# Output projection by Strassen's seven products from the third block on, prompt gates folded into w_out, and v weights streamed

## The chip, the core and the metric

The kernel runs on one core of one Trainium2 chip. The metric is the device time of one execution in microseconds (us), as the median of three runs. The engines are named as in the profile: PE is the matrix engine, PEld its loading of the stationary operand, DVE the vector engine, ACT the scalar engine, POOL the third elementwise engine, and SP the engine whose queue issues most of the DMAs.

## What is computed

One layer over 4096 prompt rows of 1024 channels (x_prompt) and over 8 x 16 sample rows (x_sample). What matters here is the frame around the mixers:

```python
mod = jax.nn.silu(c) @ w_ada + b_ada
shift, scale, gate = jnp.split(mod, 3, axis=-1)
h = rmsnorm(x, norm_g) * (1 + scale[:, None]) + shift[:, None]
z = h @ w_in                                   # 3200 columns: pool, conv, spatial-gating groups
...
vn = layernorm(v, v_norm_g, v_norm_b)          # v is one of the column groups, 384 wide
y_gmlp = gmlp_mix(u, vn, w_s, b_s)
y = jnp.concatenate([y_pool * jax.nn.silu(z_pool),
                     gb * y_conv * jax.nn.silu(z_conv),
                     y_gmlp * jax.nn.silu(z_gmlp)], axis=-1) @ w_out
return x + gate[:, None] * y, new_pool, new_conv, vn
...
y_prompt = rmsnorm(xp, final_norm_g)
```

All prompt rows share one conditioning vector, so the prompt's gate is one row of 1024 numbers; the sample rows have eight.

## The kernel before

The prompt is worked off in eight blocks of 512 rows (blocks 0 to 7), then the 128 sample rows follow as a ninth block ("dec"). Every float32 product is made of three float16 products: an operand is split into a high and a low part (`split`, L150: ACT writes the high part, DVE the low part), and `PARTS` lists the three pairs that are multiplied.

The order of the program is: input half of block i (`in_block`, or `in_dec`), preparation of the input of block i+1 (`h_plain`, `h_sums`), then the output half of block i-1 (`out_block`, L1101), and last the split of block i's result `ya` for its own output half one block later (`split_y`, L1145). So the output half of block 3 runs behind the input half of block 4, and the v product of block 5 follows it.

An input half multiplies first the v columns (`v_product`, L751: for each of four row tiles 24 matmuls of 384 columns, weights `vw` resident in SBUF), then the other columns in pairs of tiles. From block 1 (conv pairs: block 2) on these pairs use Strassen's seven products of half-sized operands (`quads`, L631): B11, T1, T2, B22, T3, B21, T4, 12 matmuls of 256 columns each, accumulated in three PSUM tiles x, y and z per pair. `gmlp_v` (L763) takes the four PSUM tiles `z_v`, normalises them on DVE and ACT and leaves `vh`, which the matmuls of `gmlp_mix` (`ps_mix`) read behind the first group of pairs.

The output half (`out_block`) computes 512 rows x 1024 columns in two column halves. For each half it opens four PSUM tiles `ps_o`, and for each of eight k tiles takes a weight tile from the stream and does 4 row tiles x 3 parts matmuls of 512 columns (L1173). DVE then does two operations per PSUM tile: times the scales and the gate (L1179), plus the residual `xr` (L1180). Row sums, a reciprocal root and the final scaling (L1189) follow, and ACT's queue stores the rows (L1190). `mid`, called between the halves, derives the scale of the next block's result. Block 7's output half (L1151) holds all 16 weight tiles and goes row tile by row tile.

Weights come through `Stream` (L196): a list of wanted tiles, loaded by SP in order into a ring of 18 slots of 256 KB, at most 16 tiles ahead of their use. A tile of w_out serves 12 matmuls before, a tile of a pair 12 matmuls too. SP issues in program order, and a load waits there for its buffer: `xt`, `xr` and the raw weights share the four tiles of the pool `xp`, which come free when the stores of `out_y` have landed.

In block 0 and block 1 the weights are split and stored to DRAM (`w_in_parts`, `w_out_parts`) for the later blocks; in block 1 also the gates are made (`ada_chunk`, `gates`: 16 tiles of w_ada through the stream). The order of instructions on each engine is made by a scheduler from the program's order; in parts of block 0 it is fixed by hand (`manual_schedule`, for SP in all of block 0).

## Time and profile before

| what | value |
|---|---|
| median of 3 runs | 1470.69 us (1470.62 to 1472.21) |
| the profiled execution's own time | 1467.08 us |
| its span, first to last instruction | 1465.3 us |
| mean granted clock of PE | 0.985 |
| PE busy | 1404.3 us (96%), 10370 matmuls |
| PEld busy | 975.9 us (67%) |
| DVE busy | 936.6 us (64%) |
| ACT busy | 585.0 us (40%) |
| HBM traffic | 214 GB/s over the span |

The span is one profiled execution; what lies around it (1.8 us) is part of the execution's time. A view by stretches gives each engine's busy time between two moments; a timeline gives groups of like instructions in order, with the idle time of the engine before them and what ended it in brackets.

### The profile page before, as it was taken

To read this page: it belongs to the slowest core of one execution; us is meant where nothing else is said; L and a number is where in the kernel's file an instruction comes from. 1 tells how busy PE (TensorE), PEld (TensorE's weight loads), DVE (VectorE), ACT (ScalarE), POOL (GpSimd) and SP (SyncE) were. 2 spreads that over 40 slices of the span, in tenths; PEclk is the share of its full clock that TensorE was granted. 3 is DMA by queue.
4 is the path that set the end of the run, shared out by engine and by line. 5 is a ranking of instruction groups with operands and counts; after the bars stand their busy time and mean duration, and the time that the engine had idled before them with its cause. 6 is when DMAs were issued, how large, how long until landed. Compare 5 with 4: busy or idle time off the path is not lost.

```text
span 1465.3 us, 26791 instructions
## 1 busy us (share of the span) xinstructions
PE 1404.3 (96%) x10370; PEld 975.9 (67%) x10370; DVE 936.6 (64%) x2073; ACT 585.0 (40%) x1166; POOL 119.6 (8%) x166
## 2 busy tenths in 40 slices
PE   5799999999999999999999999999999999999697
PEld 2454454584788658884788658874888568865663
DVE  3874696878887668465865657455845667354445
ACT  3676653553446434342533324342533234222121
POOL 0000202220020102000010002000200002000000
PEclk8999999999999999999999999999999999999999
DMA  9556737995559639685577639764776547774961
GB/s 352 207 222 230 280 110 258 343 361 163 209 182 356 219 129 330 174 279 159 213 242 200 187 116 321 194 184 158 263 214 200 155 139 243 204 214 125 230 179 58
DMA packets 155009, 315.08 MB, mean 215 GB/s; under 512 B 25217, under 2 KB 27009, under 8 KB 154881
## 3 DMA queue, kind: packets, MB, share of 16 engines
q1 hardware_dynamic: 143632, 295.28, 62.2%
q10 hardware_dynamic: 11248, 18.08, 3.6%
q8 instruction: 81, 1.33, 0.4%
q14 instruction: 48, 0.39, 0.1%
HBM read 267.06 MB, written 46.24 MB: 214 GB/s over the span
## 4 chain that ended last, share of the span: by engine, by line
PE 76%; DVE 10%; DMA 9%; ACT 2%; issue 1%; POOL 1%; SPq 0%; ACTq 0%; DVEq 0%; POOLq 0%
PE ps_o L1173 20%; PE zx L627 17%; PE zq L627 11%; PE zy L627 8%; PE z_v L757 7%; PE zz L627 5%; PE ps_o L1151 3%; DMA xt<-in_x 3%; PE z L627 2%; DVE mix L823 2%; DVE d L728 2%; DVE xr L1189 2%; DMA ws<-in_wada 1%; DMA raw<-in_win 1%; DMA ws<-w_in_parts 1%
## 5 line engine op out<-in xcount | busy, mean ns | idle before, releaser
L627 PEld LDWEIGHTS <-ws 128*128 128x128 f16 x6360 | 598.8, 98 | 114.6 <-issue 18.9
L1173 PE MATMUL ps_o<-ws,yh 128*128 128x512 f16 x1344 | 291.9, 379 | 0.0
L1173 PEld LDWEIGHTS <-yh 128*128 128x128 f16 x1344 | 131.0, 98 | 155.8
L627 PE MATMUL zy<-S,ws 128*128 128x256 f16 x1572 | 184.2, 273 | 0.0
L627 PE MATMUL zx<-A,ws 128*128 128x256 f16 x1572 | 183.4, 273 | 0.2 <-DVE np L659 0.2
L627 PE MATMUL zx<-S,ws 128*128 128x256 f16 x1440 | 168.8, 273 | 9.6 <-ACT nzg L655 6.7
L627 PEld LDWEIGHTS <-wp 128*128 128x128 f16 x1056 | 103.1, 98 | 74.8 <-issue 7.6
L757 PE MATMUL z_v<-vw,A 128*128 128x384 f16 x792 | 132.7, 330 | 1.9 <-ACT A L310 1.7
L627 PE MATMUL zq<-A,wp 128*128 128x512 f16 x528 | 117.3, 383 | 0.0
L757 PEld LDWEIGHTS <-A 128*128 128x128 f16 x792 | 77.8, 99 | 55.7 <-ACT A L310 2.5
L153 ACT ACTIVATE yh<-ya,sy 128x512 f16<-128x512 f32 x64 | 40.7, 708 | 166.2 <-PE ps_o L1173 162.5
L1179 DVE SCALAR_TENSOR_TENSOR ps_o<-ps_o,io,gate_p 128x512 f32<-128x512 f32 x56 | 40.9, 751 | 102.9 <-PE ps_o L1173 102.9
L627 PE MATMUL zz<-A,ws 128*128 128x256 f16 x852 | 101.5, 273 | 0.0
L627 PE MATMUL zq<-A,ws 128*128 128x512 f16 x288 | 62.6, 379 | 0.0
L711 POOL COPY qh<-q 128x2 f32<-128x2 f32 x24 | 6.6, 273 | 559.1 <-DVE q L710 559.1
L701 DVE SCALAR_TENSOR_TENSOR c<-q,wconv_sb,c 128x512 f32<-128x512 f32 (+1 forms) x54 | 38.0, 704 | 21.7 <-ACT c L699 21.1
L714 ACT ACTIVATE nzc<-nzc 128x512 f32<-128x512 f32 x24 | 15.1, 628 | 80.9 <-DVE nzc L659 80.8
L823 DVE SCALAR_TENSOR_TENSOR mix<-ps_mix,wsg,wsb 64x256 f32<-64x256 f32 x96 | 46.3, 482 | 1.4
L154 DVE SCALAR_TENSOR_TENSOR yh<-ya,sy,yh 128x512 f16<-128x512 f32 x64 | 44.9, 740 | 0.0
L627 PE MATMUL z<-A,ws 128*128 128x128 f16 x588 | 37.7, 228 | 5.9 <-ACT sz L1034 5.4
L725 POOL TENSOR_TENSOR pw<-pw 128x524 f32<-128x524 f32 (+5 forms) x36 | 42.6, 1183 | 8.1 <-DVE d L728 5.8
L741 POOL COPY ph<-pe 128x15 f32<-128x15 f32 x16 | 3.7, 232 | 476.6 <-ACT pe L740 476.3
(277 smaller groups left out, 1739.0 us busy)
## 6 DMA issues: line engine op xcount, KB each, us to landing
ws<-w_in_parts SPq DMA_DIRECT2D x517, 256.0 KB, 3.1
ws<-w_out_parts SPq DMA_DIRECT2D x128, 256.0 KB, 3.5
w_in_parts<-wp SPq DMA_DIRECT2D x83, 256.0 KB, 4.3
t<-in_xT SPq DMA_DIRECT2D x32, 512.0 KB, 6.0
xr<-in_x SPq DMA_DIRECT2D x32, 512.0 KB, 7.2
out_y<-xr ACTq DMA_DIRECT2D x32, 512.0 KB, 3.9
xt<-in_x SPq DMA_DIRECT2D x28, 512.0 KB, 6.1
ws<-in_wada SPq DMA_DIRECT2D x48, 256.0 KB, 5.4
```

Source lines behind the costliest of these rows:

```text
L153: nc.scalar.activation(dst_hi, src, AF.Identity, scale=s)
L154: nc.vector.scalar_tensor_tensor(dst_lo, src, s, dst_hi, ALU.mult, ALU.subtract)
L627: nc.tensor.matmul(ps, w[:, a, k, :], h[:, c, k, :], start=first and i == 0, stop=last and i == 3 * KH - 1, skip_group_check=True)
L701: nc.vector.scalar_tensor_tensor(c, at(i), wc[:, j, i:i + 1], c, ALU.mult, ALU.add)
L725: nc.gpsimd.tensor_tensor(cut(s, lo), cut(sums[-1], lo), cut(sums[-1], lo - w, -w), ALU.add)
L728: nc.vector.scalar_tensor_tensor(dv[rows], cut(sums[e], 16)[rows], state["G"]["cinv"][rows, i:i + 1], cut(pe, 16)[rows], ALU.mult, ALU.sub ...
L757: nc.tensor.matmul(ps, H[1 + k // KH][:, a, k % KH, t * P:(t + 1) * P], vw[:, e, k, :], start=i == 0, stop=i == 3 * KT - 1)
L823: nc.vector.scalar_tensor_tensor(mo[to, :, t, :], po[of, :, e, :], gc[of, hd:hd + 1], bias[of, hd, :].unsqueeze(1).broadcast_to([64, 2, P] ...
L1151: nc.tensor.matmul(ps, yh[:, a, k, t * P:(t + 1) * P], state["w"][hf][k][:, c, 0, :], start=k == 0 and i == 0, stop=k == KT - 1 and i == 2)
L1173: nc.tensor.matmul(pss[t], yh[:, a, k, t * P:(t + 1) * P], w[:, c, 0, :], start=k == 0 and i == 0, stop=k == KT - 1 and i == 2)
L1179: nc.vector.scalar_tensor_tensor(pss[t], pss[t], io[:, hf:hf + 1], gate[:, hs], ALU.mult, ALU.mult)
L1189: nc.vector.scalar_tensor_tensor(xts[t], xts[t], r[:, t:t + 1], O["fg"], ALU.mult, ALU.mult)
```

## The change

1. From block 2 on (`OUT_FAST`) the output half of a prompt block uses Strassen's seven products too (`out_fast`): operands of the result's split are seven sums of its quarters (`split_y_fast`), and weights are plain tiles or the four sums of w_out's quarters, which block 3 makes once and stores (`out_sums`). Each product has 4 k tiles x 2 row tiles x 3 parts matmuls of 512 columns. Three PSUM pairs x, y, z are accumulated across products, and DVE adds what stands in them to the residual after each product. The final row work (`out_rows`) stands behind the seventh product; in block 7 half of it stands behind the sixth.
2. The prompt's gate is multiplied into w_out in block 1 (`out_bounds`), so DVE does one operation per PSUM read where it did two. The sample rows need w_out without gates, which block 5 makes (`later`). The gates themselves are made in block 0 now. The high part of w_out's split is written by ACT, not POOL.
3. The split v weights are stored to DRAM in the first 40 us and come through the stream, eight tiles of 192 KB for each block; `v_products` goes k tile by k tile over four PSUM tiles that end together.
4. Weight jobs move: `unfold` from block 3 to block 4, `out_sums` into block 3, the plain w_out into block 5.

```diff
+    def v_products(b, H):
+
+        pss = [psum("z_v")[:, :384] for _ in range(b.tt)]
+        for k in range(KT):
+            w = stream.get()[:, :768].rearrange("p (a c) -> p a c", a=2)
+            for t in range(b.tt):
+                for i, (a, e) in enumerate(PARTS):
+                    nc.tensor.matmul(pss[t], H[1 + k // KH][:, a, k % KH, t * P:(t + 1) * P], w[:, e, :],
+                                     start=k == 0 and i == 0, stop=k == KT - 1 and i == 2)
+            stream.ahead(1)
+        return pss
...
         for i in range(3):
             cols = slice(i * P, (i + 1) * P)
             split(vw[:, 0, :, cols], vw[:, 1, :, cols], t[:, i, :].rearrange("p (k c) -> p k c", k=KT), s)
+        for k in range(KT):
+            nc.sync.dma_start(wvd[k].rearrange("p (a c) -> p a c", a=2), vw[:, :, k, :])
...
+    def out_bounds(hf, sts, gate=None):
+
+        m = sm.tile([P, 4], F32, tag="wom", name="wom", bufs=1)
+        for q, st in enumerate(sts):
+            if gate is not None:
+                nc.vector.tensor_tensor(st, st, gate.unsqueeze(1).broadcast_to([P, 2, 512]), ALU.mult)
+                nc.sync.dma_start(wofd[hf][:, 2 * q:2 * q + 2, :], st)
+            bound(m[:, q:q + 1], st, 4.0)
+        return m
...
+    def out_sums(k, a, c):
+
+        (_, s1), (_, s2) = state["O"]["inv"]
+        r11, r12, r21, r22 = a[:, 0], a[:, 1], c[:, 0], c[:, 1]
+        stt = nc.vector.scalar_tensor_tensor
...
+        nc.scalar.activation(r11, r11, AF.Identity, scale=s1)
+        nc.vector.tensor_tensor(r22, r22, r12, ALU.subtract)
+        stt(r12, r12, s2, r11, ALU.mult, ALU.subtract)
+        out(0, r12)
+        stt(r11, r22, s2, r11, ALU.mult, ALU.add)
+        out(1, r11)
+        out(2, r22, s2)
+        stt(r21, r21, s1, r11, ALU.mult, ALU.subtract)
+        out(3, r21)
...
+                if b.i == 0 and j > 0:
+                    gates(j - 1, ada_chunk(stream.get), state["O"])
...
-                if b.i == 1 and j < 2:
-                    t = ada_chunk(stream.get)
-                    out_weights(j, state["O"], *wo)
-                    if j == 0:
-                        wo = out_load(1)
-                    gates(j, t, state["O"])
...
+    def split_y_fast(ya, sy):
+
+        y11, y21, y12, y22 = ya[:, :KH, :HT], ya[:, :KH, HT:], ya[:, KH:, :HT], ya[:, KH:, HT:]
+        Ya = hop.tile([P, 4, 2, KH, HT], F16, tag="yh", name="yh")
+        Yb = hop.tile([P, 3, 2, KH, HT], F16, tag="yh2", name="yh2")
+        op = {B11: Ya[:, 0], T1: Ya[:, 1], T2: Ya[:, 2], B22: Ya[:, 3], T3: Yb[:, 0], B21: Yb[:, 1], T4: Yb[:, 2]}
+        split(op[B11][:, 0], op[B11][:, 1], y11, sy)
+        split(op[T4][:, 0], op[T4][:, 1], y22, sy)
+        nc.vector.tensor_tensor(y22, y21, y22, ALU.add)
+        split(op[T1][:, 0], op[T1][:, 1], y22, sy)
+        nc.vector.tensor_tensor(y21, y11, y21, ALU.subtract)
+        split(op[T3][:, 0], op[T3][:, 1], y21, sy)
+        nc.vector.tensor_tensor(y11, y22, y11, ALU.subtract)
+        split(op[T2][:, 0], op[T2][:, 1], y11, sy)
+        split(op[B21][:, 0], op[B21][:, 1], y12, sy)
+        nc.vector.tensor_tensor(y12, y12, y11, ALU.subtract)
+        split(op[B22][:, 0], op[B22][:, 1], y12, sy)
+        return op
...
+    def out_fast(b, op, io, xts, mid):
+
+        pss = {}
+        reads = {B11: (0, 0), T1: (1, 1), T2: (0, 1), B22: (0, 1), T3: (1, 1), B21: (0, 0), T4: (1, 0)}
+        for p in (B11, T1, T2, B22, T3, B21, T4):
+            bank = "y" if p in (T1, B22) else "z" if p == B21 else "x"
...
+            for k in range(KH):
+                w = as_parts(stream.get(), 512)
+                for t in range(2):
+                    for i, (a, c) in enumerate(PARTS):
+                        nc.tensor.matmul(pss[bank][t], op[p][:, a, k, t * P:(t + 1) * P], w[:, c, 0, :],
...
+                stream.ahead(1)
+            half, hf = reads[p]
+            hs = slice(hf * 512, hf * 512 + 512)
+            for t in range(2):
+                xt = xts[2 * half + t][:, hs]
+                nc.vector.scalar_tensor_tensor(xt, pss[bank][t], io[:, hf:hf + 1], xt, ALU.mult, ALU.add)
+            if p == T2:
+                mid()
+            if b.last and p in (B21, T4):
+                out_rows(b, xts, (2 * half, 2 * half + 1))
+        if not b.last:
+            out_rows(b, xts, range(TB))
...
     for i in range(1, NPB):
-        stream.want += in_items(i) + wod
-    stream.want += dec_items() + wod
+        stream.want += in_items(i) + out_items(i - 1)
+    stream.want += dec_items() + out_items(NPB - 1) + wosd
```

Three places show how instructions stand now. The first is DVE behind the output half of block 3, up to the first reading of the next v product. Before, from the last matmuls of `ps_o`'s second half on (`yh` is the split result of block 4, `z_v` the v product of block 5):

```order
L1179 SCALAR_TENSOR_TENSOR ps_o<-ps_o,io,gate_p 128x512
L154 SCALAR_TENSOR_TENSOR yh<-ya,sy,yh 128x512
L1180 TENSOR_TENSOR xr<-ps_o,xr 128x512
L154 SCALAR_TENSOR_TENSOR yh<-ya,sy,yh 128x512 x2
L1180 TENSOR_TENSOR xr<-ps_o,xr 128x512
L154 SCALAR_TENSOR_TENSOR yh<-ya,sy,yh 128x512
L774 BN_STATS bst<-z_v 128x6
L154 SCALAR_TENSOR_TENSOR yh<-ya,sy,yh 128x512 x4
```

The same place now, from the reading of the seventh product (`ox`) on:

```order
L1246 SCALAR_TENSOR_TENSOR xr<-ox,io,xr 128x512 x2
L161 SCALAR_TENSOR_TENSOR yh_10049<-ya,sy,yh_10049 128x1024 x2
L1200 TENSOR_TENSOR ya<-ya 128x4x256
L1219 TENSOR_SCALAR omsq_10017<-oss 128x4
L1202 TENSOR_TENSOR ya<-ya 128x4x256
L129 TENSOR_SCALAR rs_t<-omsq_10017 128x4
L133 TENSOR_SCALAR rs_y<-omsq_10017 128x4
L161 SCALAR_TENSOR_TENSOR yh<-ya,sy,yh 128x1024
L1204 TENSOR_TENSOR ya<-ya 128x4x256
L131 TENSOR_SCALAR rs_r<-rs_t 128x4
L161 SCALAR_TENSOR_TENSOR yh_10049<-ya,sy,yh_10049 128x1024
L1207 TENSOR_TENSOR ya<-ya 128x4x256
```

Two more splits of 128x1024 follow before the four `BN_STATS` of `z_v`, which stood amid the splits before and stand behind all of them now; the four scalings of `xr` (L1222) stand between them and the reading of `z_v` that frees its PSUM tiles, as L1189 did.

The second place is SP's queue around the same v product, where `xt` waits for the stores of the block before. Before:

```order
L217 DMA ws<-w_out_parts 128x1024 x16
L217 DMA ws<-w_in_parts 128x1024 x8
L295 DMA t<-in_xT 128x1024 x4
L217 DMA ws<-w_in_parts 128x1024 x10
L238 DMA xt<-in_x 128x1024
```

Now (behind the 28 weight tiles of the output half):

```order
L302 DMA t<-in_xT 128x1024
L224 DMA ws<-w_v_parts 128x768
L224 DMA ws<-w_in_parts 128x1024 x22
L245 DMA xt<-in_x 128x1024
L224 DMA ws<-w_in_parts 128x1024 x2
```

Eight loads of v weights came in, and the first `xt` stands behind 22 tiles of the next pairs where it stood behind 18.

The third place is SP's queue in the first 45 us, whose order is fixed by hand. Before (`t` is the input of block 0, the first `raw` are the v weights, the second the weights of the first conv pairs):

```order
L295 DMA t<-in_xT 128x1024 x4
L491 DMA raw_148<-in_win 128x1024 x3
L217 DMA ws<-in_wada 128x512 x16
L399 DMA raw<-in_win 128x1024 x4
L592 DMA gate_p<-in_badag 128x512 x2
```

Now:

```order
L302 DMA t<-in_xT 128x1024 x4
L497 DMA raw_147<-in_win 128x1024 x3
L224 DMA ws<-in_wada 128x512 x16
L513 DMA w_v_parts<-vw 256x1x384 x8
L405 DMA raw<-in_win 128x1024 x4
```

The eight stores of the split v weights stand ahead of the raw weights of the first conv pairs.

## Rows read from the trace of the kernel before

**Rows 1.** The page: busy time (share) and instructions of engines; chain by engine.
```profile
PE 1404.3 (96%) x10370; PEld 975.9 (67%) x10370; DVE 936.6 (64%) x2073; ACT 585.0 (40%) x1166; POOL 119.6 (8%) x166
...
PE 76%; DVE 10%; DMA 9%; ACT 2%; issue 1%; POOL 1%; SPq 0%; ACTq 0%; DVEq 0%; POOLq 0%
```

**Rows 2.** Timeline of PE behind block 4's input half: start, us, group [idle before].
```profile
839.41 20.88 PE L1173 MATMUL ps_o<-ws,yh 128*128 128x512 f16 x96
860.12 15.76 PE L757 MATMUL z_v<-vw,A 128*128 128x384 f16 x96
875.73 2.78 PE L627 MATMUL zx<-A,ws 128*128 128x256 f16 x24
...
888.83 2.78 PE L627 MATMUL zz<-A,ws 128*128 128x256 f16 x24
...
894.07 1.50 PE L816 MATMUL ps_mix<-wmix,vh 128*128 128x128 f16 x24
```

**Rows 3.** Stretches: us, PE, PEld, DVE, ACT, POOL busy, PEclk, DMA share, GB/s.
```profile
698.41:860.10 161.69, 160.51 (x1254) 121.07 (x1253) 99.72 (x209) 58.26 (x119) 10.57 (x16) 1.00 0.65 204
...
875.90:894.20 18.30, 18.30 (x171) 16.40 (x170) 14.31 (x46) 10.85 (x22) 3.29 (x6) 1.00 1.02 379
```

**Rows 4.** Timelines of PE and DVE in blocks 0 and 1, around the gates.
```profile
114.69 0.16 PE L145 MATMUL ps_sum<-asum,ones 128*128 128x1 bf16 x1 [3.11 <-DVE asum L143]
228.58 1.92 PE L273 MATMUL ps_ada<-ws,c_sb 128*32 128x512 f32 x16
231.29 1.98 PE L594 MATMUL ps_gate<-t_ada,ex 128*128 128x512 f32 x4 [0.67 <-ACT t_ada L276]
...
113.10 0.38 DVE L556 MEMSET st_ws<- 64x384 f32 x1 [7.03 <-DMA st_ws<-in_wsT]
```

**Rows 5.** Groups by line, DVE: forms, count, busy us, mean ns, idle before.
```profile
L1179 DVE SCALAR_TENSOR_TENSOR ps_o<-ps_o,io,gate_p 128x512 f32<-128x512 f32 x56 | 40.9, 751 | 102.9 <-PE ps_o L1173 102.9
L347 DVE TENSOR_TENSOR t<-t 128x1024 f32<-128x1024 f32 x7 | 8.5, 1217 | 0.0
L154 DVE SCALAR_TENSOR_TENSOR vw<-raw,w_s,vw 128x1024 f16<-128x1024 f32 x3 | 3.7, 1282 | 1.2 <-ACT vw L153 1.2
L774 DVE BATCH_NORM_STATS2 bst<-z_v 128x6 f32<-128x384 f32 x33 | 18.2, 551 | 1.4 <-PE z_v L757 1.4
...
L133 DVE TENSOR_TENSOR rs_q<-rs_q,rs_y 128x4 f32<-128x4 f32 x45 | 8.9, 197 | 1.2
...
L133 DVE TENSOR_TENSOR rs_q<-rs_q,rs_y 128x2 f32<-128x2 f32 x48 | 7.4, 154 | 0.6
```

**Rows 6.** Timeline of DVE behind the same output half.
```profile
872.89 4.87 DVE L1189 SCALAR_TENSOR_TENSOR xr<-xr,rs_r,fgain 128x1024 f32<-128x1024 f32 x4
...
880.40 1.26 DVE L786 TENSOR_SCALAR v<-z_v,va,vb 128x384 f32<-128x384 f32 x2
...
885.86 1.26 DVE L786 TENSOR_SCALAR v<-z_v,va,vb 128x384 f32<-128x384 f32 x2
```

**Rows 7.** Timeline of SP's queue, the first xt of block 5.
```profile
877.28 0.33 SPq L238 DMA_DIRECT2D xt<-in_x  x1
```

**Rows 8.** Timelines of SP's queue, DVE and ACT in the first 53 us.
```profile
31.34 2.36 SPq L399 DMA_DIRECT2D raw<-in_win  x4
...
34.59 3.68 DVE L154 SCALAR_TENSOR_TENSOR vw<-raw,w_s,vw 128x1024 f16<-128x1024 f32 x3 [1.16 <-ACT vw L153]
...
52.83 1.04 ACT L162 ACTIVATE junk<-raw 128x1024 bf16<-128x1024 f32 x1
```

**Rows 9.** Input half of the sample rows: PE, SP's queue, and its stretch (columns of Rows 3).
```profile
1384.76 0.62 PE L807 MATMUL ps_mix<-wmix_s,vh 128*128 128x128 f16 x3 [4.34 <-ACT gc L1022]
...
1392.70 1.97 PE L627 MATMUL z<-A,ws 128*128 128x128 f16 x17 [5.45 <-ACT sz L1034]
...
1374.48 0.33 SPq L1109 DMA_DIRECT2D xr<-in_x  x1
...
1348.07:1405.63 57.56, 45.57 (x684) 43.14 (x683) 30.24 (x80) 17.71 (x49) 3.46 (x7) 0.88 0.96 236
```

202 lines of the change are left out of this document (123 added, 79 removed).

## The prediction

> **What bounds the kernel now.** I read the page first: PE is busy for 96% of the span, every other engine for less than two thirds, and the chain that ended last runs through PE for 76% [rows 1]. A busy PE need not be a PE without slack, so the second view is PE's timeline where the change sits, behind the input half of block 4 [rows 2]: an output half is two groups of 96 matmuls, the v product follows without a gap, and the first pairs of block 5 follow that. No group there has an idle time in brackets. From the start of the second half (839.41) to the start of the v product (860.12) 20.71 us pass, so one matmul of 512 columns costs 20.71/96 = 0.216 us from start to start; the 20.88 of the row holds the modelled end of the last one as well. The third view is the stretch of a whole block: 161.69 us with PE busy for 160.51, at a granted clock of 1.00, the 2.4 GHz level [rows 3]. The middle blocks are therefore PE's issue rate and little else; a matmul that goes away there shortens the run by its spacing, unless something new is late. Only at the start [rows 4, 8] and in the input half of the sample rows [rows 9] does PE wait for others.
>
> **What is removed from PE.** Before, an output half is 2 x 8 x 4 x 3 = 192 matmuls; seven products are 7 x 4 x 2 x 3 = 168. Six blocks (2 to 7) lose 24 each: 144 x 0.216 = **31.1 us**. Size and stationary operand of a matmul stay, the clock is at its upper level there, so I take the spacing as it is.
>
> The Trainium skill, TensorE: Matmul & The Clock Gate, section Back-to-back issue gap, gives two figures for the spacing of matmuls of 512 columns: about 216 ns by its formula for the bare gap, and about 131 ns as measured in a stream with weight loads between. By the second the saving would be 144 x 0.131 = 18.9 us, an estimate; the trace has 0.216 in just such a stream, so it bears out the first.
>
> **Gates, from block 1 to block 0.** In block 1 two chunks cost 1.92 + 1.98 us each on PE plus a wait of 0.67 [rows 4], together 9.1 us. They cost the same in block 0, but the first one now stands where PE waited 3.11 us for a chain that began with a late DMA of `st_ws` (DVE idle 7.03 us) [rows 4]. The PE work of 3.9 us covers most of that wait, and the DMA moves back by two issues only. I take **-2.4 us**, from -3.1 (all covered) to +1 (the two loads ahead of `st_ws` push the chain by as much as they fill).
>
> **DVE and ACT at the seam between two blocks.** This is where new waits can come. Per read of PSUM DVE has one operation of 0.75 us [rows 5] where it had two, and 14 reads where it had 8; that is even. But the split of `ya` grows: seven splits of 128x1024, nearest row 1.28 us on DVE, and four additions, nearest row 1.22 us [rows 5]. The order shows what of it cannot begin early: T4's operand overwrites a tile that the seventh product still reads, and T1, T3, T2 and B22 depend on `ya` as changed after it. So behind the seventh product stand two reads (1.5 us), six splits (7.7), four additions (4.9) and some eight small operations (about 1.3): 15.4 us on DVE. PE meanwhile does the rest of the v product, 15.6 us in all. DVE reaches `BN_STATS` when PE ends v, not before.
>
> From there the same chain as now runs: statistics, small operations, four scalings of `xr` (4.87 us [rows 6]), then the reads that free `z_v`. Before they began at 880.40 and 885.86 [rows 6], 4.7 and 10.1 us behind the end of v (875.73 [rows 2]), because half the statistics were done during v. Now I get 4 x 0.55 for the statistics, some 35 small ones at 0.15 to 0.2 [rows 5] and 4.87: 13 us for the first pair, about 21 for the second. PE wants PSUM again at the pair's `zz`, 13.1 us behind v's end (888.83 against 875.73), and `vh` at `ps_mix`, 18.3 us behind it (894.07) [rows 2]. PSUM holds eight tiles; x, y and `z_v` fill it, so `zz` waits for the first pair of reads: 0 to 2 us. The order puts half of `ps_mix` behind the next group of matmuls, which covers 2.6 us of the second delay; 1 to 2 us remain. Against it stands about 1.2 us of idle PE per block now (161.69 less 160.51 [rows 3]), part of which a wait upstream absorbs. I take 1.5 us at each of four seams (before blocks 4 to 7) and 1 us for blocks 1 to 3, where only v's order changes: **+7 us**, from 0 to +20 (5 us a seam, if ACT and DVE hand each split over without overlap: the `vw` row shows 1.2 us idle before the first of three [rows 5]).
>
> **Inside the output half** nothing should wait. Product T2 accumulates on what DVE must have read after B11, with T1 (5.2 us) between; likewise the others. Two reads of 0.75 us fit, and the order puts them in time.
>
> **Streams.** A block loads 12 more tiles of w_out and eight of v, 4.7 MB on 204 GB/s x 161.69 us = 33 MB [rows 3]; in 156 us that makes about 242 GB/s, below the 379 that the first pairs of a block reach [rows 3]. A w_out tile is used up in 1.3 us instead of 2.6, which is what pairs do now. The critical place is `xt`, which stops SP until `out_y` has landed, at 877.28 [rows 7], 1.5 us after v's end, with 18 tiles in the ring. Now v has used its tiles, and the stores start some 9 us later against v's end; 22 tiles are issued ahead of `xt`, about 8 used, so 14 remain, 18 us of work at 1.3. I cost it at nothing; if the cover goes, each missing tile costs its transfer, 256 KB at 379 GB/s, 0.7 us.
>
> **The rest.** *Start:* the v stores wait for the split, which ends at 38.3 [rows 8], and the raw weights behind them are issued near 43 (eight issues at some 0.6) instead of 31.34. They are first needed at 52.83 [rows 8]; 1.6 + 2.1 MB from 38.3 at 379 GB/s land by 49. +0.5 us, 0 to 4. *Weight jobs:* `out_sums` adds 4 x 8 operations of 0.75 = 24 us to DVE in block 3, plain w_out some 12 us in block 5; DVE has 62 us free in a block [rows 3]. PE may meet them at a few PSUM reads: +2 us, 0 to 8. *Sample rows:* here DMA is the limit, share 0.96 at 236 GB/s over 57.56 us while PE works 45.57, with waits of up to 4.34 and 5.45 us [rows 9]. Eight v tiles are 1.57 MB, 6.7 us at that rate. But SP's stop at `xr` (issued at 1374.48 [rows 9]) now has two tiles of the pairs behind it instead of ten, and the wait of 5.45 that followed it should go for the most part: +2 us, from -3 to +8. *End:* the row work of block 7 is hidden behind the sample rows' projection, as before: 0.
>
> **Sum.** -31.1 - 2.4 + 7 + 0.5 + 2 + 2 = -22.0 us. The profiled execution took 1467.08 (span 1465.3 and 1.8 around it), so 1445.1; the median of the runs shown is 3.6 above it, which makes **1449 us**.
>
> **Rivals.**
> 1. *The gain comes whole.* No new wait at the seams or in the sample rows, only the matmuls and the gates count: 1470.7 - 33.5 = 1437, to 1441 with small ones. For it: PE has no gap in the rows of the seam and its queue can pass other work; against it: the count of 15.4 us against 15.6. Chance 0.22.
> 2. *The forecast*, some waits, 1441 to 1456. Chance 0.58.
> 3. *DMA or DVE eats half.* Block 3 or 5 or the ring starves, 10 to 25 us in sum: 1456 to 1467.8. For it: a DMA share of 1.02 at the seam already [rows 3]; against it: 14 tiles in hand. Chance 0.12.
> 4. *A removed matmul is worth less than its row.* If the 24 that go from a block had been closer together than the others, their spacing might be that of the v product, 15.61/96 = 0.163 us [rows 2]: 144 x 0.163 = 23.4, 7.7 us less than I take, so 1457. Against it: 96 of one kind without a gap. Chance 0.02. The Trainium skill's 131 ns (TensorE: Matmul & The Clock Gate, Back-to-back issue gap) would put it later still, at 1461, an estimate.
> 5. *Slower.* The reads that free `z_v` come so late that `zz` waits about 9 us at each of four seams, 36 us: every split is handed from ACT to DVE and back, 1.2 us [rows 5] for each of six, which puts 7 us on the 15.4, and the chain behind it the rest. At 1.5 us a seam the forecast is 22 us faster, so from 7 us a seam on there is no gain; at 9 the time is 1479. Against it: ACT is idle for most of that time (58 us busy in a block [rows 3]). Chance 0.04.
> 6. *No difference*, gains and waits even, within 0.2% (3 us, about what a measurement of this kernel can tell from no change): 0.02. That the change doesn't do what it says is no case: the order shows 168 matmuls in an output half.
>
> **How the numbers follow.** Faster by over 0.2% are 1 to 4: 0.94. The range runs from 1438 to 1460: it leaves out the best part of case 1 (about 0.1), two thirds of case 3 (0.08) and cases 5 and 6, and takes in the ends of the start and the sample rows.
>
> **What would show it.** PE's timeline in the middle: output halves of 36.3 us; blocks of about 156 to 158 us. Seam: idle PE before `zz` or the next `zx`, put down to DVE `v` or ACT `vh`, 1 to 3 us. Block 0: no 3.1 us before `ps_sum`. Sample rows' input half: 57 to 63 us. The prediction is wrong if blocks 4 to 7 are longer than 160 us, if `ws` loads stop PE in the middle, or if DVE's share at the seam is below nine tenths.

## The result, and the profile after

The changed kernel takes **1454.91 us** (median of four, 1451.86 to 1458.41) where the kernel before took 1470.87 beside it: a ratio of 0.989, 95% interval 0.9867 to 0.9914. That is 16 us faster, where 22 were forecast. The profiled execution took 1451.86 us, its span is 1450.1, so all of the accounting below is made between two spans: 1465.3 and 1450.1, 15.2 us apart.

The page of the changed kernel, first part, answers to [rows 1]: busy time, share and instructions of each engine.

```profile
PE 1374.6 (95%) x10228; PEld 961.5 (66%) x10228; DVE 998.7 (69%) x2113; ACT 637.9 (44%) x1228; POOL 110.5 (8%) x150
```

PE lost 29.7 us of work, and DVE and ACT gained 62 and 53. PE's share fell by a point all the same: the time went down by half of what left PE. The next view tells where the rest stayed. It cuts the span of the changed kernel at the ends of the v products, with the columns of [rows 3]: from the v product of block 3 to that of block 4, then of block 5, 6 and 7, and, behind a line that is left out, the input half of the sample rows without its v product, block 7's output half, and the end.

```profile
551.90:715.34 163.44, 156.00 (x1230) 118.67 (x1229) 121.73 (x237) 71.57 (x138) 11.59 (x16) 1.00 0.83 279
715.34:875.49 160.15, 157.40 (x1233) 119.34 (x1230) 108.55 (x220) 65.97 (x126) 11.40 (x16) 0.99 0.78 249
875.49:1033.07 157.58, 155.59 (x1233) 118.67 (x1232) 115.95 (x235) 78.74 (x150) 10.88 (x16) 1.00 0.83 292
1033.07:1189.99 156.92, 155.37 (x1230) 118.57 (x1229) 104.52 (x208) 61.16 (x118) 12.61 (x18) 1.00 0.76 234
...
1351.20:1393.85 42.65, 28.91 (x419) 27.78 (x418) 17.51 (x49) 6.30 (x25) 3.25 (x6) 0.80 1.06 261
1393.85:1430.14 36.29, 36.29 (x173) 16.46 (x170) 14.38 (x40) 5.04 (x14) 0.00 (x0) 1.00 0.87 294
1430.14:1450.10 19.96, 10.58 (x73) 6.03 (x71) 14.73 (x40) 4.63 (x11) 3.42 (x3) 0.84 0.34 133
```

The line 1393.85 is the cleanest: an output half alone, 36.29 us of PE without a gap. It took 41.37 before; the four lines above hold such a half each beside other work. Cut in the same way, the kernel before gives 162.16, 161.72, 161.65, 161.79, then 166.20 up to the end of the sample rows' v product (161.21 after), 40.26, 41.37 and 18.30. Taking 5.18 us for each of the six halves (24 x 0.216), the two spans compare like this:

| part | forecast | found |
|---|---|---|
| six output halves, 144 matmuls | -31.1 | -31.1 |
| from the start to the end of v in block 3 | -0.9 | +0.1 (551.85 to 551.90) |
| block 3, apart from its half | +1 | +6.5 (162.16 to 163.44, and 5.18) |
| blocks 4 to 7, apart from their halves | +7 | +5.2 (651.36 to 635.86, and 4 x 5.18) |
| input half of the sample rows | +2 | +2.4 |
| last half beyond 5.18, and the end | 0 | +1.8 |
| sum | -22.0 | -15.2 (rounded parts) |

The gain came whole. What was given back is 15.9 us where 9.1 were forecast, and most of the difference stands in block 3. The second line flatters this execution a little: in eight other profiles of kernels with the same first blocks v of block 3 ends at 552.8 to 558.9, so part of the 3 us by which the median lies above the profiled execution may stand there.

Three places were read closely before the experiments. **The seam between blocks 3 and 4** comes first, in five timelines of the changed kernel (start, us, group, [idle before <- what ended it]): SP's queue, ACT, POOL, DVE and PE. The v product ends at 715.34.

```profile
722.98 0.33 SPq L245 DMA_DIRECT2D xt<-in_x  x1
...
722.40 0.44 ACTq L1223 DMA_DIRECT2D out_y<-xr  x1
731.06 1.06 ACT L246 ACTIVATE xt<-xt 128x1024 f32<-128x1024 f32 x1 [3.87 <-DMA xt<-in_x]
732.12 1.12 ACT L789 COPY pe<-np 128x512 f32<-128x512 f32 x2
...
732.93 1.06 POOL L774 TENSOR_TENSOR pw<-pe 128x526 f32<-128x526 f32 x1
...
725.38 1.26 DVE L848 TENSOR_SCALAR v<-z_v,va,vb 128x384 f32<-128x384 f32 x2
734.03 1.65 DVE L777 SCALAR_TENSOR_TENSOR d<-pw,cinv_sb,pe 64x512 f32<-64x512 f32 x1 [3.26 <-POOL pw L774]
735.60 1.25 DVE L848 TENSOR_SCALAR v<-z_v,va,vb 128x384 f32<-128x384 f32 x2
738.06 1.89 DVE L851 TENSOR_TENSOR vh<-v,vh 128x384 f16<-128x384 f32 x2
...
740.00 0.67 PE L878 MATMUL ps_mix<-wmix,vh 128*128 128x128 f16 x8 [1.75 <-DVE vh L851]
```

Read it from the bottom up. PE stands 1.75 us for `vh` (2.74 us with two smaller waits ahead of it, 0.49 and 0.50). `vh` needs the second pair of v's reads, which starts 20.3 us behind v's end. The first pair starts 10.0 us behind it. What stopped DVE between the two is `d`, which stands ahead of the second pair in its queue and waited 3.26 us for POOL's `pw`. `pw` waited for `pe` on ACT, and ACT stood 3.87 us for `xt`. `xt` was issued 7.6 us behind v's end, right behind the last store of `out_y`; before it was 1.55 us behind it [rows 2, 7]. In the kernel before the order on DVE is the other way round: the second pair is at 885.86 [rows 6], and this line of its timeline, `d`, stands behind it.

```profile
892.03 1.65 DVE L728 SCALAR_TENSOR_TENSOR d<-pw,cinv_sb,pe 64x512 f32<-64x512 f32 x1 [1.21 <-POOL pw L725]
```

**Block 3** holds the job that makes the four sums of w_out's quarters (`out_sums`). PE's and then DVE's timeline of the changed kernel:

```profile
591.37 4.09 PE L676 MATMUL zx<-A,ws 128*128 128x256 f16 x36 [1.98 <-DVE nzg L708]
608.49 1.47 PE L676 MATMUL zx<-A,ws 128*128 128x256 f16 x12 [1.23 <-DVE nzg L708]
...
607.35 0.69 DVE L661 TENSOR_TENSOR st_ws<-st_ws 128x512 f32<-128x512 f32 x1 [3.29 <-DMA st_ws<-w_out_folded]
607.96 0.48 DVE L708 SCALAR_TENSOR_TENSOR nzg<-zx,w_i,nzg 128x256 f32<-128x256 f32 x1
```

The job's operation (L661) stands in DVE's queue ahead of a read of PSUM (L708) and waits 3.29 us for its own load; the read needs nothing of it and is late by as much. PE has other matmuls for part of that time and waits 1.23 us. With three more waits for reads on ACT and DVE (1.77, 1.98 and 2.41 us) PE stands 7.4 us in this block, against one wait of 1.33 before.

**The sample rows** have their waits at another place than before. ACT's queue with its stores, then PE, then what the DMA view says of the stretch from 1347 to 1394:

```profile
1372.37 0.37 ACT L1113 ACTIVATE gc<-z,w_i 128x128 f32<-128x128 f32 x1 [5.66 <-DMA out_y<-xr]
1378.03 0.39 ACTq L1120 DMA_DIRECT2D out_ncs<-q  x1
1378.47 0.40 ACT L748 ACTIVATE c<-q,wconv_sb 128x128 f32<-128x128 f32 x1 [5.73 <-DMA out_y<-xr]
...
1369.72 0.77 PE L1151 MATMUL ps_pl<-d,wpool_sb 128*128 128x128 f32 x2 [5.62 <-DVE d L777]
...
DMA packets 10138, 12.63 MB, mean 269 GB/s; under 512 B 4953, under 2 KB 5081, under 8 KB 10131
```

Half of the packets are under 512 bytes. Most of those are the new pool and conv states, stored in pieces of 60 and 8 bytes, and each of these stores is issued by ACT. Around them ACT is idle for 5.7 us, twice here.

### The profile page after: what moved, and what is told of

Its sections match the earlier page's. It is cut to its first block, busy times and chain, and to the rows that moved or that the text cites. A ratio compares the mean times of both kernels' runs of the same rounds, so it can differ in the third digit from the quotient of the medians.

```text
span 1450.1 us, 27021 instructions
## 1 busy us (share of the span) xinstructions
PE 1374.6 (95%) x10228; PEld 961.5 (66%) x10228; DVE 998.7 (69%) x2113; ACT 637.9 (44%) x1228; POOL 110.5 (8%) x150
## 4 chain that ended last, share of the span: by engine, by line
PE 47%; DVE 7%; DMA 4%; ACT 1%; issue 1%; POOL 0%; ACTq 0%; DVEq 0%
PE zx L676 15%; PE ox L1238 9%; PE zy L676 7%; PE oy L1238 4%; PE zz L676 4%; PE z_v L819 2%; PE z L676 2%; PE oz L1238 2%; DVE xr L1222 1%; DMA xt<-in_x 1%; DVE yh L161 1%; DMA out_y<-xr 1%; DMA ws<-w_in_parts 1%; DVE d L777 1%; DVE vh L851 0%
## 5 line engine op out<-in xcount | busy, mean ns | idle before, releaser
L1238 PEld LDWEIGHTS <-yh 128*128 128x128 f16 x1008 | 98.1, 98 | 116.2
L1238 PE MATMUL ox<-ws,yh 128*128 128x512 f16 x576 | 128.6, 379 | 0.0
L819 PE MATMUL z_v<-ws,A 128*128 128x384 f16 x696 | 115.1, 326 | 0.0
L819 PEld LDWEIGHTS <-A 128*128 128x128 f16 x696 | 68.1, 98 | 46.0
L160 ACT ACTIVATE yh<-ya,sy 128x1024 f16<-128x1024 f32 (+1 forms) x58 | 57.6, 1025 | 63.3 <-PE ox L1238 17.0
L1305 PE MATMUL ps_o<-ws,yh 128*128 128x512 f16 x384 | 83.6, 379 | 0.0
L161 DVE SCALAR_TENSOR_TENSOR yh<-ya,sy,yh 128x1024 f16<-128x1024 f32 (+1 forms) x58 | 64.4, 1134 | 7.7 <-ACT yh L160 7.6
L1217 ACT ACTIVATE junk<-xr 128x1024 bf16<-128x1024 f32 x32 | 33.4, 1045 | 81.0 <-DVE xr L1246 56.1
L1305 PEld LDWEIGHTS <-yh 128*128 128x128 f16 x384 | 37.4, 98 | 44.2
L1246 DVE SCALAR_TENSOR_TENSOR xr<-ox,io,xr 128x512 f32<-128x512 f32 x48 | 34.1, 748 | 46.8 <-PE ox L1238 46.8
L1238 PE MATMUL oy<-ws,yh 128*128 128x512 f16 x288 | 64.3, 379 | 0.0
```

Of the source, the lines that this page charges most:

```text
L160: nc.scalar.activation(dst_hi, src, AF.Identity, scale=s)
L161: nc.vector.scalar_tensor_tensor(dst_lo, src, s, dst_hi, ALU.mult, ALU.subtract)
L819: nc.tensor.matmul(pss[t], H[1 + k // KH][:, a, k % KH, t * P:(t + 1) * P], w[:, e, :], start=k == 0 and i == 0, stop=k == KT - 1 and i == 2)
L1217: nc.scalar.activation(junk.bitcast(BF16), xts[t], AF.Square, accum_out=ss[:, j:j + 1])
L1238: nc.tensor.matmul(pss[bank][t], op[p][:, a, k, t * P:(t + 1) * P], w[:, c, 0, :], start=first and k == 0 and i == 0, stop=k == KH - 1 and ...
L1246: nc.vector.scalar_tensor_tensor(xt, pss[bank][t], io[:, hf:hf + 1], xt, ALU.mult, ALU.add)
```

## The experiments

My theory: the removed matmuls give all of their 31 us, and what can be won back is three separate waits: `xt` behind the stores at the seams, the job in block 3, and the small stores in the sample rows (of which only +2.4 us are new). The rival that speaks against it: the split itself, DVE's 15.4 us behind the seventh product, or its pressure on everything, eats the gain.

**1. The change without the seven products.** All of the change stays, but every output half is the plain one.

```diff
-OUT_FAST = 2
+OUT_FAST = 8
```

> Every block's output projection is the plain one (OUT_FAST = 8); folded gates, streamed v weights, the moved weight jobs and the tiles of w_out sums that nobody reads stay. Theory: the 144 matmuls are worth their spacing, 31.1 us, and most of what the changed kernel lost again sits behind the longer split at the seams before blocks 4 to 7 (about 7 us of waits and 2 us at a lower clock), which goes here: 1455 + 31 - 9 = about 1477 us. Rival 1, the loss has nothing to do with the split (streams, weight jobs, sample rows): 1455 + 31 = 1486. Rival 2, a removed matmul is worth only 0.163 us: at most 1455 + 23 = 1478 without, and 1469 with, the waits; the output halves of the two traces tell these apart, 41.4 us here against 36.3.

Measured: 1.0100 [1.0077, 1.0123], 1483.17 us. The rest of the change alone makes the kernel slower by 1%, 14.7 us, nearly what the changed kernel gave back. By the ratio that is 1486 where the changed kernel takes 1455: rival 1, and not the theory. Against the changed kernel it is 2.1%, 31 us (24 to 38 by the two intervals), which is 144 x 0.216. The stretch of block 4 and the last output half of this kernel:

```profile
722.95:886.53 163.58, 160.88 (x1256) 121.03 (x1254) 98.85 (x210) 62.41 (x127) 10.14 (x16) 1.00 0.69 224
...
1420.46:1461.92 41.46, 41.46 (x196) 18.80 (x194) 8.17 (x23) 3.80 (x11) 0.00 (x0) 1.00 0.55 189
```

The half is 5.17 us longer, and the middle block has 2.7 us of idle PE although the seven operands are not made there: before, it was 1.2 [rows 3]. So a loss of this size comes without the longer split; something else in the change causes it.

**2. Without the job of block 3 as well.** The four sums are not made (no product uses them here).

```diff
-            if i == 3:
+            if i == 33:
```

> As the kernel with plain projections in every block, and in addition the job of block 3 that makes the sums of w_out is left out (nobody reads them there). Theory: that job, 32 operations of 0.75 us on DVE, is what makes PE wait four times for PSUM reads in block 3 (7.4 us against 1.3 before): 5 to 6 us less than the kernel with the job. Rival: DVE has room in block 3, and those waits come from elsewhere (streams): within 1 us of the kernel with the job.

Measured: 1.0078 [1.0053, 1.0104], 1480.23 us: the job is worth some 3 us here, inside the spread of the two intervals and between the theory and its rival.

**3. And with v resident.** From the kernel of 2, v's weights stay in SBUF as before, are not stored and do not pass through the stream.

```diff
-        for k in range(KT):
-            nc.sync.dma_start(wvd[k].rearrange("p (a c) -> p a c", a=2), vw[:, :, k, :])
...
-            w = stream.get()[:, :768].rearrange("p (a c) -> p a c", a=2)
+            w = state["vw"][:, :, k, :]
...
-        return wvd + [s for pi in ORDER for s in pair_items(i, pi)]
+        return [s for pi in ORDER for s in pair_items(i, pi)]
```

> Plain projections in every block, without block 3's job, and the v weights stay resident (no stores of them at the start, no tiles of them streamed); the v product keeps its new order, tile by tile of the weights. Theory: streaming v costs little by itself, up to 1 us a block in the ring: against the same kernel with v streamed (1480 where before took 1468) up to 7 us less. Rival: the stream costs nothing, and the 12 us between that kernel and the one before come from the gates, the new order of v and the row work at the end: within 2 us of it.

Measured: 0.9971 [0.9954, 0.9987], 1465.57 us. Streaming v costs 1.07%, 15.7 us, in a kernel without the split, more than twice what the theory allowed. First the kernel of 2, then this one, each with block 5's stretch (from v's end to the next) and ACT's first use of `xt` in block 5:

```profile
881.29:1044.41 163.12, 160.98 (x1256) 121.08 (x1255) 105.79 (x223) 75.37 (x151) 9.98 (x16) 1.00 0.77 263
...
889.04 1.06 ACT L246 ACTIVATE xt<-xt 128x1024 f32<-128x1024 f32 x1 [3.15 <-DMA xt<-in_x]
```

```profile
874.57:1035.74 161.17, 160.65 (x1256) 121.09 (x1255) 106.50 (x223) 75.96 (x151) 10.36 (x16) 1.00 0.75 257
...
878.39 1.06 ACT L246 ACTIVATE xt<-xt 128x1024 f32<-128x1024 f32 x1 [0.53 <-DMA xt<-in_x]
```

Between the two profiles 4.6 us lie in the sample rows (44.73 and 40.15 for their input half behind v), 6.9 in blocks 3 to 7 and 3.7 in block 2. ACT can use `xt` 7.75 us behind v's end with the stream (889.04 - 881.29) and 3.8 without it, and waits 3.15 us against 0.53. That eight more tiles ahead of `xt` delay it fits this; it was not isolated in these two.

**4. `xt` later in program order.** In blocks 4 to 6 its load, its first use and the weight job are issued behind ACT's `vh` and `pe`, so neither is queued behind it.

```diff
+                if b.i >= 4 and f is pools:
+                    with tc.issue_after(state["vh_ins"].ins), tc.issue_after(state["pe_ins"].ins):
+                        load_next()
+                        next(jobs, None)
+                    continue
```

> The changed kernel, with ACT's statistics of the next block's rows (xt) queued behind the copies pe and the casts vh of the same block, in blocks 4 to 6; nothing is left out. Theory: at the seams PE waits for vh because of a chain that starts with the late landing of xt: xt, ACT, pe, POOL pw, DVE d, DVE v, vh, ps_mix. Taken out of ACT's queue, the waits of 2.7, 2.0 and 1.6 us before blocks 4 to 6 shrink below 0.5 us each and the clock does not fall in block 4 (2 us): 5 to 8 us less, 1447 to 1450. Rival: the split's 15.4 us of DVE work delay v themselves, whatever ACT does: within 1 us of the changed kernel, with the same waits.

Measured: 0.985 [0.9833, 0.9868], 1445.94 us, 5.9 below the changed kernel by the ratios (0 to 12 by the two intervals, so the trace has to carry it). The same seam as above (v's end at 715.86), now on DVE and PE, and block 5's stretch:

```profile
732.99 1.25 DVE L848 TENSOR_SCALAR v<-z_v,va,vb 128x384 f32<-128x384 f32 x2
...
737.39 0.62 PE L878 MATMUL ps_mix<-wmix,vh 128*128 128x128 f16 x8 [0.17 <-DVE vh L851]
...
871.43:1027.02 155.59, 155.42 (x1233) 118.70 (x1231) 116.07 (x235) 78.92 (x150) 11.04 (x16) 1.00 0.84 296
```

`pe` (at 729.11) no longer waits for a DMA and stands 3.5 us earlier against v's end, v's second read 3.1 us earlier, and PE's wait is 0.17. Blocks 4 to 6 take 155.57, 155.59 and 155.92 with PE busy for 155.4: nothing is left at these seams, although DVE does all of the split's work as before. That settles the seams against the rival.

**5. The job of block 3 behind the reads.** Its operations are issued behind a DVE and an ACT read of PSUM.

```diff
-                next(jobs, None)
+                if b.i == 3:
+                    with tc.issue_after(state["dve"].ins), tc.issue_after(state["act"].ins):
+                        next(jobs, None)
+                else:
+                    next(jobs, None)
```

> The changed kernel; in block 3 each piece of the job that makes the sums of w_out is queued on DVE and ACT behind the last reads of PSUM of the pair that stands ahead of it in the program. Nothing is left out, and the number of operations stays. Theory: PE's waits of 1.8, 2.0, 1.2 and 2.4 us in block 3 come from pieces of the job that stand in DVE's and ACT's queues ahead of those reads, some of them waiting for their own load (3.3 us): block 3, 163.4 us in the changed kernel, gets 3 to 6 us shorter. Rival: it is the amount of work on DVE (122 us busy of 163) that delays the reads, wherever it stands: within 1 us.

Measured: 0.9854 [0.9839, 0.9869], 1449.04 us, some 5 us better (0 to 11 by the two intervals). Block 3's stretch:

```profile
554.89:712.77 157.88, 155.52 (x1230) 118.70 (x1229) 121.10 (x237) 72.24 (x138) 11.93 (x16) 1.00 0.83 289
```

157.88 against 163.44 (160.94 in the second profile of the changed kernel, experiment 9), with one wait of over 1 us left (2.33, at 589.05) and with the same operations on DVE (121 us): the job cost by where it stood, 3 to 5.5 us, and not by its 24 us of work.

**6. Without the state stores.** Four stores are left out; the outputs for new states and `vn` of the sample rows are not written.

```diff
-                nc.scalar.dma_start(nvs, vn)
...
-            nc.scalar.dma_start(ncs[:, j], q[:, :, ND:])
...
-            nc.scalar.dma_start(nps[:, i], pe[:, :, 17:])
...
-        nc.scalar.dma_start(npp, G["ph"])
```

> The changed kernel, with the small stores of the sample rows' states left out (out_ncs, out_nps, out_npp, out_nvs: four outputs are not written). Theory: in the sample rows' input half ACT stands about 5.6 us at each of its stores while the DMA queues are full, and PE's waits of 5.6, 2.3 and 4.1 us follow from that: the stretch from the end of v to the output half gets 6 to 10 us shorter. Rival: the weights' transfers bound this stretch (DMA share 1.06), and the small stores ride along: at most 2 us less.

Measured: 0.9788 [0.9765, 0.981], 1436.38 us, 15 us better.

**7. The states packed.** Both states are gathered in SBUF by POOL and stored once each at the end, in pieces of 192 and 960 bytes.

```diff
+        pk_c = con.tile([P, 3, NB, 2], F32, name="pk_c")
+        pk_p = con.tile([P, 2, NB, HIST], F32, name="pk_p")
...
-            nc.scalar.dma_start(ncs[:, j], q[:, :, ND:])
+            nc.gpsimd.tensor_copy(pk_c[:, j], q[:, :, ND:])
...
-            nc.scalar.dma_start(nps[:, i], pe[:, :, 17:])
+            nc.gpsimd.tensor_copy(pk_p[:, i], pe[:, :, 17:])
...
+        nc.scalar.dma_start(ncs, pk_c)
+        nc.scalar.dma_start(nps, pk_p)
```

> The changed kernel with the sample rows' conv and pool states gathered by five small POOL copies and stored in two transfers at the end of the input half, with packets of 192 and 960 bytes in place of 5,000 packets of 8 and 60. Nothing is left out. Theory: the 17.7 us that the input half lost against the kernel without those stores are the price of the small packets in the DMA queues, so this gets 13 to 17 us of them back: 1438 to 1442 on a chip where the changed kernel takes 1455. Rival: it is that ACT and the queues stand at any store there, whatever its packets: under 5 us.

Measured: 0.9798 [0.9784, 0.9813], 1440.69 us: 13.5 us better with all outputs there. The sample rows' input half, without the stores and then packed:

```profile
1352.72:1377.62 24.90, 24.33 (x419) 23.97 (x418) 16.64 (x43) 6.23 (x23) 4.16 (x6) 1.00 1.02 377
```

```profile
1352.49:1381.54 29.05, 24.68 (x419) 24.05 (x418) 16.15 (x43) 6.22 (x23) 5.15 (x9) 1.00 1.03 380
...
DMA packets 6120, 12.63 MB, mean 366 GB/s; under 512 B 934, under 2 KB 1190, under 8 KB 6113
```

42.65 us (40.42 in the second profile of the changed kernel) become 24.90 and 29.05. The DMA share is above one in all three, but 380 GB/s go through it instead of 261, and the granted clock is 1.00 instead of 0.80. The last line is the DMA view of the packed kernel from 1347.5 to 1382: the same 12.63 MB as in the changed kernel from 1347 to 1394. There the packets of the queues of SP and ACT took 79.8% and 25.0% of 47 us, here 81.9% and 18.3% of 34.5 us: 49 us of the 16 engines became 35 for the same bytes. So what I took for a limit of the weights' traffic in [rows 9] (share 0.96 at 236 GB/s) was in the main the price of small pieces; most likely in the kernel before too, where the same stores stand, but no run left them out there. ACT still stands around stores in the packed kernel (7.01 us ahead of `gc` at 1364.51). The edit also moved the stores to the end of the input half, and what that gave by itself is not separated.

**8. `st_ws` first in block 0.** Its load is issued ahead of the gates' chunks.

```diff
+                mst = mixer_load(False) if b.i == 0 and j == 1 else None
                 if b.i == 0 and j > 0:
                     gates(j - 1, ada_chunk(stream.get), state["O"])
```

> The changed kernel with the load of the mixer's weights (st_ws) in block 0 issued ahead of the gates' loads instead of behind them. Nothing is left out. Theory: the gates did not cover PE's wait in block 0 because st_ws was issued 2.4 us later and landed 6.6 us after its issue instead of 4.4, so the chain behind it moved by 4.8 us; issued first, it lands some 4 us earlier, and PE's wait of 2.2 us before ps_sum goes: 1.5 to 2.5 us less up to the v product of block 1. Rival: that wait hangs on DVE's and ACT's work for the gates, not on the load: no change of block 0 within 0.5 us.

Measured: 0.9911 [0.9896, 0.9927], 1456.72 us, no gain. PE's timeline ahead of block 1's v product in this kernel:

```profile
201.93 13.39 PE L823 MATMUL z_v<-ws,A 128*128 128x384 f16 x71 [3.26 <-ACT A L333]
```

The wait before `ps_sum` is gone, as it should (it starts at 118.12); this wait of 3.26 us has come instead, behind ACT's preparation of the next block. The gain moved to the next thing that was late.

**9. The changed kernel once more,** without an edit, for its spread.

> The changed kernel once more, unchanged, as the measure for the kernels beside it: 1452 to 1458 by its own runs. If the spread of 6.5 us between its executions comes from the first two blocks, this profile differs from the first one ahead of block 2's v product (386.9 there) and by less than 1 us in each block behind.

Measured: 0.9913 [0.9882, 0.9944], 1456.83 us (1450.74 to 1460.14); the gain is confirmed, at the small end. In its profile block 3 takes 160.94 and the sample rows' half 40.42, 2.5 and 2.2 us less than in the first one, with nothing changed; its start is that much later. I had expected the stretches to repeat more closely. Single stretches of this kernel are known to some 2 or 3 us, which is why block 3's +6.5 above is between 4 and 6.5.

**10. Edits 4, 5, 7 and 8 together,** with the sample rows' loads of statistics and mixer behind the casts, and the old pool states loaded in one transfer.

```diff
+                with tc.issue_after(state["vh_ins"].ins), tc.issue_after(state["pe_ins"].ins):
+                    r_dec = load_stats(nb)
+                    st_dec = mixer_load(True)
...
-                    nc.sync.dma_start(pes[:, i, :, 1:16], stp[:, i])
+                nc.sync.dma_start(pk_p, stp)
```

> The changed kernel with all four: statistics of the next rows behind the casts on ACT (also before the sample rows), the job of block 3 behind the reads of PSUM, the mixer's load first, the states packed (and the old pool state loaded in one transfer of 960-byte packets). If the four places are independent their gains add: 6 + 4 + 2 + 14 = 26 us less than the changed kernel, about 1429. If one hides behind another, for instance the sample rows' wait moves to the weights' transfers once the stores are gone, 1434 to 1440.

Measured: 0.9723 [0.9706, 0.9739], 1430.37 us, close to the sum for independent places.

**11. The same without edit 8.**

```diff
-                mst = mixer_load(False) if b.i == 0 and j == 1 else None
...
-                    state["G"]["mixer"] = mixer(state["G"], False, mst)
+                    state["G"]["mixer"] = mixer(state["G"], False)
```

> The kernel with all four edits less the mixer's load first, which took away PE's wait of 2.2 us in block 0 and brought one of 3.3 us ahead of block 1's v product (ACT came later to A). Theory: that edit cost what it gave and more, so without it the v product of block 2 ends 3 to 5 us earlier (389 instead of 393.4 in the trace) and nothing else moves: 1425 to 1428 on a chip where the other took 1430. Rival: those 4 us are the spread of the first two blocks between executions (386.9 to 393.6 so far, with and without the edit): 1430.

Measured: 0.975 [0.9716, 0.9784], 1431.43 us (1424.3 to 1434.97). The median misses the expected one; 10 and 11 can't be told apart. Both beat the kernel before by 38 to 40 us and the changed one by 21 to 28 by the ratios, against its two measurements. The stretches of block 0 up to v of block 1 and of block 4 in the profile of 11:

```profile
61.00:215.24 154.24, 148.15 (x775) 72.12 (x773) 110.02 (x259) 99.04 (x178) 11.81 (x16) 1.00 0.76 260
...
710.32:865.86 155.54, 155.39 (x1231) 118.62 (x1230) 108.38 (x220) 65.84 (x126) 11.55 (x16) 1.00 0.79 256
```

**12. Kernel 11 with v resident,** for which the ring shrinks to make room.

```diff
-    RING, LOOK = 18, 16
+    RING, LOOK = 13, 11
...
-            w = stream.get()[:, :768].rearrange("p (a c) -> p a c", a=2)
+            w = state["vw"][:, :, k, :]
```

> The best kernel so far (statistics behind the casts, block 3's job behind the reads, states packed; 0.975 of the kernel before), with the v weights resident again and the ring of weight tiles cut from 18 to 13 tiles to make room for them; nothing is left out. Theory: with ACT's queue free of xt the blocks 4 to 6 are at PE's own time already (155.6 us), so the stream of v costs nothing there; what residency can give is the 3.7 us of block 2 and the 1 to 5 us of the start and the sample rows: 5 to 8 us less. Rival: a ring of 13 tiles (some 17 us of PE's work) no longer covers the stop of SP's queue at the next rows' loads, and PE waits for weights at each seam: 3 to 15 us more.

Measured: 0.9911 [0.9895, 0.9928], 1452.93 us, 23 us later than 11, and at a place that neither theory named. Block 0 and block 4 of this kernel, and PE in block 0:

```profile
61.00:238.82 177.82, 157.37 (x780) 75.64 (x778) 110.57 (x262) 100.03 (x178) 11.11 (x16) 0.94 0.61 212
...
730.30:885.84 155.54, 155.40 (x1231) 118.68 (x1230) 108.41 (x220) 65.84 (x126) 11.54 (x16) 1.00 0.74 246
...
134.97 0.19 PE L152 MATMUL ps_sum<-asum,ones 128*128 128x1 bf16 x1 [7.05 <-DVE asum L150]
```

The whole loss is in block 0 (177.82 against 154.24), where SP, in the order fixed by hand, stands for free slots of the shorter ring: the first eight loads of the gates' weights take it 16.01 us from 82.28 on (3.76 in kernel 11), and `st_ws` is issued at 126.81 instead of 110.66. Block 4 takes 155.54 in both: once `xt` is out of the way, streaming v costs nothing there. What of the 15.7 us from 3 stood in the middle blocks is therefore no price of the traffic, but of what it delays; for block 2 and the sample rows that is not shown.

## Why the prediction was right, point by point

**The forecast case came, at its late end.** 1454.91 lies in the second case (1441 to 1456), within the range, and the sign is right; the gain is 16 us instead of 22.

**144 x 0.216 was right.** The first two groups of an output half on PE's timeline of the changed kernel, each one product's 24 matmuls, start 5.18 us apart:

```profile
823.60 5.34 PE L1238 MATMUL ox<-ws,yh 128*128 128x512 f16 x24
828.78 5.34 PE L1238 MATMUL oy<-ws,yh 128*128 128x512 f16 x24
```

That is 0.216 each, as in [rows 2]; experiment 1 gives the same from the other side: (41.46 - 36.29)/24 = 0.215. Rival 4 (0.163) is out. The Trainium skill, TensorE: Matmul & The Clock Gate, Back-to-back issue gap, gives 131 ns for this in a stream with weight loads; the trace disagrees by 65%, and its formula for the bare gap, about 216 ns, is what this stream runs at.

**The gates gave about nothing instead of -2.4.** In block 0 they cost what I counted, 6.68 us beyond the start (9.1 - 2.4), but by luck: a wait that I had counted as gone still stands there, and what made up for it is the clock. The stretch around that wait, in the kernel before and in the changed one (columns of [rows 3]):

```profile
95.00:125.00 30.00, 26.89 (x136) 13.93 (x135) 12.52 (x36) 20.89 (x37) 0.37 (x2) 0.94 0.56 194
...
95.00:125.00 30.00, 27.01 (x147) 13.54 (x145) 14.18 (x29) 17.57 (x32) 0.83 (x2) 1.00 0.68 241
```

A granted clock of 0.94 over 30 us is 1.8 us lost, in the profile of the kernel before, where PE had stood for 3.11 us in it; no term of mine held that. In eight other profiles with these first blocks the way from the first v product to block 1's is 0.3 to 3.4 us longer than in this one, and three of them have the 0.94 as well. Block 1 gave back 6.36, not 9.1: it has three new waits, 0.97, 0.44 and 1.65 us. PE's timeline, with ACT's row that explains the second wait shown:

```profile
119.48 0.18 PE L152 MATMUL ps_sum<-asum,ones 128*128 128x1 bf16 x1 [2.21 <-DVE asum L150]
...
261.89 1.06 ACT L169 ACTIVATE junk<-st_wo 128x1024 bf16<-128x1024 f32 x1 [2.16 <-DVE st_wo L622]
...
263.29 0.16 PE L152 MATMUL ps_sum<-asum,ones 128*128 128x1 bf16 x1 [0.97 <-DVE asum L150]
```

The first was 3.11 [rows 4] and I had it covered by PE's new work. But what it waits for, `st_ws`, moved back as well: issued at 111.16 instead of 108.73, and landed 6.6 us later instead of 4.4. The failed step is "the DMA moves back by two issues only". The 0.97 comes from work that I didn't count at all: the fold multiplies w_out by the gate on DVE, eight operations of 1.23 us (L622), and the bound waits for them. The cause of the 1.65 stays open.

**The seams: the size is right, the reason is not, so the size is luck.** I forecast 1.5 us a seam, from a split that keeps DVE busy up to v's end. DVE's count held: `BN_STATS` starts at 714.21 with v's end at 715.34, the first reads are 10.0 us behind v's end (13 forecast), and `zz` at 728.44 waits for nothing. The waits are at the next group and `ps_mix`, 2.74, 2.0 and 1.55 us before blocks 4, 5 and 6, and they come from the second pair of reads, which stands behind `d` in DVE's queue, and `d` behind `xt`. The step that failed is "I cost it at nothing": I asked of `xt` only what SP's queue holds behind it (tiles, of which there were enough), not who waits for `xt` itself on ACT, and what stands behind that. Experiment 4 shows it: with `xt` behind the casts the three blocks reach PE's floor, with the split as it is. The second pair starts 20.3 us behind v's end where I forecast about 21, but in experiment 4 it starts at 17.1: the agreement is chance, since the 20.3 hold a wait of 3.26 us that I had not counted. What the split does is make the stores of `out_y`, and `xt` with them, late: the first store is issued 3.5 us behind v's end (718.81), and before it was issued 1.5 us ahead of it (874.21).

**The job in block 3 is the mis-sized term.** I gave it 1 us (2 with block 5's, 0 to 8) since DVE has room; it cost some 5 by the ratios (0.989 against 0.9854 in experiment 5) and 3 to 5.5 by block 3's stretches. Room on an engine doesn't help a read that is queued behind an operation whose load has not landed.

**The sample rows: +2 was met with +2.4,** on a wrong reading. Their input half takes 59.95 us (17.3 up to v's end, and 42.65) where it took 57.56, within the 57 to 63 forecast, but the limit was not the bytes of the weights. Experiment 7 shows that 13.6 us of it (11.4 against the second profile) are the small stores, which were there before the change; the 17.7 of experiment 6 hold the larger store of `vn` too. The wait of 5.45 behind SP's `xr` went, as I said, and one of 5.62 for `d` stands there now, behind a store on ACT. The Trainium skill, DMA: Bandwidth & Descriptors, Specifications, names 512 bytes as the least piece for full rate; the trace agrees, with 269 GB/s over a stretch with 4,953 packets below that and 366 over the same bytes with 934.

**The end cost 1.7, not 0.** The row work of block 7 is not all hidden now: half of it, in this line of DVE's timeline, stands ahead of the sample rows' second read, which starts at 1440.92.

```profile
1437.50 3.50 DVE L1222 SCALAR_TENSOR_TENSOR xr<-xr,rs_r,fgain 128x1024 f32<-128x1024 f32 x2
```

Against the test I set: blocks 5 and 6 are within "about 156 to 158"; block 4 is at 160.15 (159.40 in the second profile), just over the line at which I called the prediction wrong; block 7's 161.21 holds the first products of the sample rows, and up to these it is 4.99 us shorter than before. No `ws` load stops PE in the middle. DVE's share is 0.95 while v runs (14.81 of 15.64 us), but from v's end to `ps_mix` at 740 it is 0.82 (20.2 of 24.66 us), below the nine tenths I had set as the sign of a wrong mechanism. That sign came, and rightly: DVE stands there for `pw`, as in this stretch (columns of [rows 3]).

```profile
730.00:735.00 5.00, 5.00 (x54) 4.55 (x52) 1.71 (x4) 3.33 (x6) 2.14 (x3) 1.00 1.03 407
```

## What to carry to other kernels

Where PE is the bound, a matmul that goes away is worth its spacing in the row, and the working belongs into what then becomes late. For every load that moves, ask not only what the queue that issues it holds up, but which engine's queue stands on its landing and whose feeds are behind that: two such places cost some 11 us here, with room on every engine, and were mended by order alone. Some 13 us more came from larger pieces in a place that was slow before the change. A DMA share near one is a limit of bytes only if the GB/s are near what other stretches reach (261 against 380 at a share above one, here); otherwise look at the sizes of the packets.
